# Feed forward 0 on inputs that hold the token scale, its relu on ScalarE, and a quarter of the S5 table pieces made in embedding stage 0

## Chip, cores and metric

The kernel runs on one core of one Trainium2 chip. The metric is the device time of one execution in microseconds (us): of three runs of the kernel before, the median is 2734.46 (2730.87 to 2736.14). One execution was taken with the hardware profiler; all views come from it.

Engines are called as in the profile: PE is TensorE's matmul, PEld its weight load, DVE is VectorE, ACT is ScalarE, POOL is GpSimd, and SP is SyncE, which here only issues DMAs.

## Reference

A decoder of two layers on 1024 tokens with 1024 channels. What matters here is the feed forward part of layer 0, the embedding part behind it, and the S5 mixer of layer 1, whose tables are made from parameters alone:

```python
def rms_norm(x, g):
    return x * lax.rsqrt(jnp.mean(x * x, axis=-1, keepdims=True) + RMS_EPS) * g

def sqrelu_mlp(hn, ffn_up, ffn_down):
    return jnp.square(jax.nn.relu(hn @ ffn_up)) @ ffn_down

for i in range(DEPTH):
    h = h + mix_fns[i % 2](rms_norm(h, norm_mix[i]), *mix_params[i])   # 0: RWKV and conv, 1: S5
    h = h + sqrelu_mlp(rms_norm(h, norm_ffn[i]), *ffn[i])
    gate = jax.nn.sigmoid(rms_norm(h, norm_ple[i]) @ ple[i][0])
    h = h + (p[i] @ ple[i][1]) * gate
```

In `rms_norm` the factor of a token (the token scale, `rstd` in the kernel) is one number per token; the gain `g` is one number per channel. The S5 mixer builds, per group, powers of `lam_bar` times `b_bar` and `c` (`s5_mixer` of the reference); the kernel keeps them as tables in DRAM.

## The kernel before

Channels lie on partitions and tokens along the free dimension, in two halves of 512 tokens (`hf` 0 and 1). `h[j][hf]` is a tile of 128 channels by 512 tokens. A product in float32 is made of three matmuls (`mm3`, L161): each operand is split into a high part (`prh`, `whi`, `uwh`, `hidh`) and the rest (`prl`, `wlo`, `uwl`, `hidl`), and high x high, high x rest and rest x high are added up in PSUM. ScalarE casts the high parts; DVE or POOL subtracts for the rest.

**The stages** in the trace are: mixer 0 (0 to 719 us), feed forward 0 (719 to 1500), embedding stage 0 (1500 to 1616), the S5 mixer with its gates (to 1912), feed forward 1 (to 2570) and embedding stage 1 with the output.

**Feed forward** (`ffn`, L238). In feed forward 0 and 1 the order of PE is the order in which the code issues matmuls; the order on the other engines is made by the scheduler. The work is cut into blocks of 8 steps. A block holds one group of up products (`u_run`, tile `ps_up`, 24 matmuls) and one group of down products (`d_run`, L348): seven products of Strassen's kind in the order X, Z, X, Y, X, Y, X, three matmuls each into `ps_dnx`, `ps_dny`, `ps_dnz`. Behind each product DVE adds the tile to the residual (L365; `h<-h,...` and `ha<-ha,...`, as the two halves are named in the profile). There is one tile for X, so the next X product waits until that addition has read it. There are 60 blocks with both groups, and a plain tail of four.

Beside them, at steps given by small tables of numbers, run the operations that prepare a later block:

- the up weights: `u_load` (SP, L261), the cast `u_hi` (ACT, L265) and the rest `u_lo` (POOL, L268);
- the down weights: `d_load` (SP, L276), four sums of blocks in `d_sums` (POOL, L281 to L284), the cast `d_hi` (ACT, L288) and the rest `d_lo` (DVE, L291), at the four steps of `FFN_D`;
- the operands of the down products (`operands`, L315): `relu()` reads `ps_up`, takes the maximum with 0 and multiplies with the token scale on DVE (L319); the squares are ACT's (L322, L323); four differences of squares (L333, one of them on POOL) are cast by ACT (L335), and the rests (L327) are DVE's, where one goes to POOL.

So the up products of feed forward 0 and 1 run on inputs that have the gain but not the token scale, which the relu adds. The scale of half 0 is known before feed forward 0 begins (`r0`); that of half 1 is computed in its first steps.

**The inputs of feed forward 0** are made by `done` in `prep` (L170): ACT casts h times gain (`prh`, L180), DVE makes the rest (`prl`, L181), sixteen pairs, called from `inputs` in `hook`.

**The S5 tables** are also made in feed forward 0: small operations on DVE first (`s5_tables`), then 32 pieces, a new one every `S5_EACH` = 12 steps. A piece (`s5_piece`, L1110) takes on POOL CL, tmp, their sum, sk and kt (L1126, L1127, L1133, L1158, L1160); on DVE two products and their sum (L1130, L1132, L1135); on PE two transposes into `ps_bl` (L1145) and two matmuls into `ps_k` (L1153); on ACT two copies and `brep`; and four DMAs to DRAM, three of them on SP (s5w from CL twice, L1140, and `toep` from kt, L1166). To each piece belongs a phase (`s5_phases`, L1190): four POOL operations (L1199 to L1203) on one buffer, and a DMA on SP (L1205). For every eight pieces there is one `s5_powers` on POOL, for every four one `s5_front` with its loads on SP, two transposes into `ps_c` and six small DVE operations.

**Embedding stage 0** (`ple`, L423) multiplies with the gate weights (tile `ps_g`), loads weights by SP (L148), casts them on ACT (L151) and takes their rest on DVE (L152). `side` is a list of generators, of which some are advanced behind each finished tile; before, it is empty. Here PE's order, too, is the scheduler's.

Of the kernel before, what the change touches and what calls it, by code (L numbers as in the profile page):

```python
# [5 lines left out]
F32 = mybir.dt.float32  # L6
F32R = mybir.dt.float32r
AF = mybir.ActivationFunctionType
ALU = mybir.AluOpType
# [3 lines left out]
P = 128  # L13
T = 1024
D = 1024
ND = D // P
H = 512
# [3 lines left out]
S5_START, S5_PREP, S5_AT, S5_EACH = -24, 1, 88, 12  # L21
# [7 lines left out]
FFN_D = (0, 2, 5, 7)  # L29
# [32 lines left out]
class Trunk:  # L62
# [107 lines left out]
    def prep(self, gain, split=True, eng=None, known={}, late=False):  # L170
# [4 lines left out]
        def done(j, hf):  # L175
            nc = self.nc
            s = self.hv(j, hf)
            if split:
# [10 lines left out]
        return st, done  # L189

# [19 lines left out]
    def rstd_steps(self, *accs, pool=None, tag="m"):  # L210
# [22 lines left out]
        yield out  # L233

# [3 lines left out]
    def ffn(self, l, xn, rstd, done, hook):  # L238
# [54 lines left out]
        def u_run(k):  # L293
# [8 lines left out]
            for hf in first:  # L302
# [12 lines left out]
        def operands(k, s, n, ps, hf, st, plain):  # L315
            r = st["f%d" % n] = self.np_.tile([P, H], F32, tag="sq", name="r_up", bufs=4)

            def relu():
                V.scalar_tensor_tensor(r, ps, 0.0, rstd[hf], ALU.max, ALU.mult)  # L319
# [573 lines left out]
    def s5_tables(self, pool, sp, keep_p):  # L893
# [167 lines left out]
        sq, rj = t("sq", (2, 64)), t("rj", (2, 64))  # L1061
        for k in range(9):
            o = lv[:, k - 2] if k >= 2 else (rj, ri)[k]
# [46 lines left out]
    def s5_piece(self, pc, pool):  # L1110
# [19 lines left out]
        V.tensor_mul(BL, bcc(LR[:, :, 0:8], 8), bck(Bb[0], 8))  # L1130
        yield
        V.tensor_mul(tmp3, bcc(LI[:, :, 0:8], 8), bck(Bb[1], 8))  # L1132
# [453 lines left out]
    def build(self, layers=(0, 1), stop=None):  # L1586
        tc, nc = self.tc, self.nc
        from contextlib import ExitStack
        with ExitStack() as st:
# [28 lines left out]
            for l in range(2):  # L1618
# [9 lines left out]
                with ExitStack() as s2:  # L1628
# [3 lines left out]
                    if l == 0:  # L1632
                        def tables():
                            with tc.tile_pool(name="s5tmp", bufs=1, reuse_waits="tile") as tp:
                                yield from self.s5_tables(tp, s5q, s5p)
                            t5 = s2.enter_context(tc.tile_pool(name="s5tab", bufs=1, reuse_waits="tile"))
                            self.kt = t5.tile([P, NG, 240], F32, name="kt")
                            nc.gpsimd.memset(self.kt, 0.0)
                            self.t5 = t5
                            yield  # L1640

                        def lazy(f, n):

                            yield from f(n, self.t5)

# [12 lines left out]

                        def hook(at, ffn_in=st, ffn_done=done):
                            at(-6, 2, lambda: inputs(ffn_in, ffn_done))  # L1660
                            at(-5, 6, lambda: next(ffn_in["r"]))
                            at(-4, 4, lambda: scale1(ffn_in))
                            def start(s):
# [5 lines left out]
                            for n in range(64 // NG):  # L1669
                                s0 = S5_AT + S5_EACH * n  # L1670
                                gs = [(lazy(self.s5_piece, n), S5_STEPS), (lazy(self.s5_phases, n), S5_PH)]
                                if n % 8 == 0:
                                    gs.append((lazy(self.s5_powers, n // 8), S5_POW))
                                if NG * n % 8 == 0:
                                    gs.append((lazy(self.s5_front, NG * n // 8), S5_FRONT))
# [77 lines left out]
```

## Time and profile before

| what | us |
|---|---|
| median of three runs | 2734.46 |
| the profiled execution, its own time | 2731.33 |
| the span of its records | 2729.6 |
| mean granted clock of PE | 0.978 |
| feed forward 0, first ps_up to the last block's first ps_dnz | 719.4 to 1472.4 |
| feed forward 1, the same two | 1912.7 to 2562.0 |
| embedding stage 0, ps_g | 1499.9 to 1615.9 |

The profiled execution lies inside the runs' range. A window's row gives for each engine the busy time and, in brackets, the count of instructions, then PE's granted clock as a share of full speed, the DMA engines' busy share and GB/s. A group's row gives busy time and the mean of one in ns, then the engine's idle time right before, with what ended it. A wait's row gives the sum, the number and the longest.

### The profile page before, as it was taken

What the parts mean: (1) busy time and instruction counts of PE and PEld (TensorE: products, weight loads), DVE (VectorE), ACT (ScalarE), POOL (GpSimd) and SP (SyncE); (2) the same over time, 40 slices, a digit from 0 to 9 for tenths busy, and PEclk for the clock granted to TensorE, in tenths of its full rate; (3) what the DMA queues carried; (4) which work ended last, traced back from release to release, by engine and by line L of the source; (5) the groups of instructions that cost most, each with busy time, mean ns of one, the idle gap of its engine ahead of it and who ended that gap; (6) DMA issues with size and microseconds to landing.
All of it is one profiled execution on the core that took longest, in us unless ns stands there. A gap on an engine that the chain in (4) does not pass through costs nothing.

```text
span 2729.6 us, 46656 instructions
## 1 busy us (share of the span) xinstructions
PE 2589.0 (95%) x18781; PEld 2068.6 (76%) x18781; DVE 1873.7 (69%) x2684; ACT 980.3 (36%) x1635; POOL 1172.6 (43%) x1516
## 2 busy tenths in 40 slices
PE   8998999999889989999999997999999999999998
PEld 6776777777667767777777876788788888888786
DVE  6664666663897788888888549523577787777854
ACT  4344444443422223333334336413333232233432
POOL 5444343443468895555554107311334334343400
PEclk9998999999989999999999989999999999999999
DMA  4223221321212223222222225211111111111121
GB/s 113 60 63 106 71 64 45 107 68 63 80 49 70 84 81 85 76 80 77 79 76 64 77 74 155 74 47 47 43 55 47 55 51 51 54 48 55 47 74 62
DMA packets 273428, 189.04 MB, mean 69 GB/s; under 512 B 33038, under 2 KB 256508, under 8 KB 273212
## 3 DMA queue, kind: packets, MB, share of 16 engines
q1 hardware_dynamic: 264336, 174.50, 21.8%
q10 hardware_dynamic: 7516, 7.10, 0.8%
q0 software_dynamic: 1360, 4.46, 0.5%
q8 instruction: 147, 2.41, 0.4%
q14 instruction: 69, 0.57, 0.1%
HBM read 156.92 MB, written 29.10 MB: 68 GB/s over the span
## 4 chain that ended last, share of the span: by engine, by line
PE 51%; DVE 6%; POOL 6%; issue 3%; DMA 1%; ACT 1%; POOLq 0%; SPq 0%; ACTq 0%; DVEq 0%
PE ps_dnx L362 10%; PE ps_up L163 6%; PE ps_up L165 6%; PE ps_up L164 6%; PE ps_dny L362 5%; PE ps_dnz L362 2%; PE ps_gl L163 2%; PE ps_gl L164 2%; PE ps_gl L165 2%; PE ps_g L163 2%; PE ps_g L165 2%; PE ps_g L164 2%; DVE ha L365 1%; POOL zs L1276 1%; DVE hidl L327 1%
## 5 line engine op out<-in xcount | busy, mean ns | idle before, releaser
L163 PE MATMUL ps_up<-prh,uwh 128*128 128x512 f32 x1024 | 407.4, 398 | 1.3 <-ACT prh L180 1.3
L164 PE MATMUL ps_up<-prl,uwh 128*128 128x512 f32 x1024 | 406.5, 397 | 1.7 <-DVE prl L181 1.6
L165 PE MATMUL ps_up<-prh,uwl 128*128 128x512 f32 x1024 | 406.9, 397 | 0.5 <-POOL uwl L268 0.5
L268 POOL TENSOR_TENSOR uwl<-uraw,uwh 128x512 fp32r<-128x512 f32 x136 | 184.4, 1356 | 187.9 <-ACT uwh L265 185.7
L281 POOL TENSOR_TENSOR draw<-draw 128x128 f32<-128x128 f32 x120 | 68.5, 571 | 402.0 <-DMA draw<-in_l_ffn_down_dram 354.6
L362 PE MATMUL ps_dnx<-hidh,whi 128*128 128x512 f32 x480 | 199.2, 415 | 43.9 <-DVE ha L365 30.1
L164 PEld LDWEIGHTS ps_up<-prl,uwh 128*128 128x128 f32 x1024 | 194.4, 190 | 49.5 <-DVE prl L181 4.8
L163 PEld LDWEIGHTS ps_up<-prh,uwh 128*128 128x128 f32 x1024 | 195.0, 190 | 47.1 <-ACT prh L180 1.8
L165 PEld LDWEIGHTS ps_up<-prh,uwl 128*128 128x128 f32 x1024 | 194.7, 190 | 46.0 <-POOL uwl L268 0.9
L365 DVE TENSOR_TENSOR h<-h,ps_dnx 128x512 f32<-128x512 f32 x240 | 164.3, 684 | 73.5 <-PE ps_dnx L362 72.6
L152 POOL TENSOR_TENSOR wlo<-wraw,whi 128x1024 fp32r<-128x1024 f32 x66 | 158.3, 2399 | 123.4 <-ACT whi L151 119.7
L202 POOL TENSOR_TENSOR acc<-acc,sq 128x512 f32<-128x512 f32 x70 | 105.0, 1507 | 220.8 <-ACT sq L201 217.7
L265 ACT CAST uwh<-uraw 128x512 fp32r<-128x512 f32 x136 | 84.3, 620 | 321.3 <-PE ps_up L164 307.9
L362 PE MATMUL ps_dnx<-hidl,whi 128*128 128x512 f32 x480 | 191.1, 398 | 4.6 <-DVE hidl L327 4.6
L362 PE MATMUL ps_dnx<-hidh,wlo 128*128 128x512 f32 x480 | 190.6, 397 | 0.5 <-DVE wlo L291 0.5
L163 PE MATMUL ps_z<-prh,whi 128*128 128x512 f32 x416 | 179.3, 431 | 7.4 <-ACT whi L151 6.6
L365 DVE TENSOR_TENSOR ha<-ha,ps_dnx 128x512 f32<-128x512 f32 x240 | 163.4, 681 | 24.1 <-PE ps_dnx L362 24.1
L165 PE MATMUL ps_z<-prh,wlo 128*128 128x512 f32 x416 | 166.9, 401 | 6.6 <-POOL wlo L152 6.5
L151 ACT CAST whi<-wraw 128x1024 fp32r<-128x1024 f32 x104 | 108.8, 1047 | 172.6 <-PE ps_z L164 59.4
L164 PE MATMUL ps_z<-prl,whi 128*128 128x512 f32 x416 | 165.7, 398 | 0.9 <-DVE prl L488 0.9
L322 ACT ACTIVATE hidh<-r_up 128x512 fp32r<-128x512 f32 x98 | 62.0, 632 | 278.5 <-DVE r_up L319 276.5
L327 DVE TENSOR_TENSOR hidl<-r_up,hidh 128x512 fp32r<-128x512 f32 x188 | 153.3, 828 | 12.7 <-ACT hidh L335 6.9
(441 smaller groups left out, 6340.5 us busy)
## 6 DMA issues: line engine op xcount, KB each, us to landing
uraw<-in_l_ffn_up_dram SPq DMA_DIRECT2D x128, 256.0 KB
draw<-in_l_ffn_down_dram SPq DMA_DIRECT2D x120, 256.0 KB
wraw<-in_l_w_in_dram SPq DMA_DIRECT2D x52, 512.0 KB
s5w<-s5w SPq DMA_DIRECT2D x32, 384.0 KB
wraw<-in_l_w_out_dram SPq DMA_DIRECT2D x16, 512.0 KB
wraw<-in_l_ple_gate_dram SPq DMA_DIRECT2D x16, 512.0 KB
wraw<-in_l_glu_w_dram SPq DMA_DIRECT2D x16, 512.0 KB
toep<-kt SPq DMA_DIRECT2D x32, 240.0 KB
```

Source lines behind the costliest of these rows:

```text
L151: nc.scalar.copy(hi[:, :n], raw[:, :n])
L152: self.lo_engine().tensor_sub(lo[:, :n], raw[:, :n], hi[:, :n].bitcast(F32))
L163: nc.tensor.matmul(ps, wh, xh, start=start, stop=False)
L164: nc.tensor.matmul(ps, wh, xl, start=False, stop=False)
L165: nc.tensor.matmul(ps, wl, xh, start=False, stop=stop)
L202: (eng or nc.vector).tensor_add(acc, acc, sq)
L265: A.copy(uw[m][0], raws["u"])
L268: nc.gpsimd.tensor_sub(uw[m][1], raws["u"], uw[m][0].bitcast(F32))
L281: G.tensor_add(raw[:, 4], raw[:, 0], raw[:, 2])
L327: return lambda: eng.tensor_sub(st[nm][1], t, st[nm][0].bitcast(F32))
L362: nc.tensor.matmul(ps, w[:, a], v, start=id(ps) not in begun, stop=n == 2, skip_group_check=True)
L365: V.tensor_add(hv, hv, ps)
```

## The change

**Inputs that hold the scale.** A new helper `scaled` makes an input as xs = h x gain x scale (DVE), a cast of it (ACT) and a subtraction (DVE). Half 0 gets its inputs this way from the start. Half 1 has them plain for the first four up groups; once its scale is known, `again` makes its eight input pairs a second time into the same tiles. Where the inputs hold the scale, `relu()` is one ACT operation without a scale, in feed forward 0 alone.

**S5 pieces.** A piece begins every 16 steps and not 12, 24 of them in feed forward 0. The last eight, with one set of powers and two fronts, are passed to embedding stage 0 as `side`, with tiles of their own (and a second clearing of kt). `FFN_D` becomes (0, 0, 3, 7). In `s5_piece` the two product tiles trade places, so that BL is written one step later.

```diff
-S5_START, S5_PREP, S5_AT, S5_EACH = -24, 1, 88, 12
+S5_START, S5_PREP, S5_AT, S5_EACH, S5_FFN = -24, 1, 88, 16, 24
-FFN_D = (0, 2, 5, 7)
+FFN_D = (0, 0, 3, 7)
...
-            if split:
+            if split and hf in known:
+                st["xn"][hf][j] = self.scaled(s, gain, j, known[hf])
+            elif split:
...
+    def scaled(self, s, gain, j, rstd, xn=None):
+        nc = self.nc
+        xn = xn or self.pair(self.prp, [P, H], "pr")
+        t = self.np_.tile([P, H], F32, tag="sq", name="xs", bufs=4)
+        nc.vector.scalar_tensor_tensor(t, s, self.c(gain, j), rstd, ALU.mult, ALU.mult)
+        nc.scalar.copy(xn[0], t)
+        nc.vector.tensor_sub(xn[1], t, xn[0].bitcast(F32))
+        return xn
...
-                        operands(k, FFN_RELU[hf != first[0]], 2 * q + hf, ps, hf, st, m >= NU - 4)
+                        operands(k, FFN_RELU[hf != first[0]], 2 * q + hf, ps, hf, st, m >= NU - 4, l == 0 and (hf == 0 or m >= 4))
...
             def relu():
-                V.scalar_tensor_tensor(r, ps, 0.0, rstd[hf], ALU.max, ALU.mult)
+                if scaled:
+                    A.activation(r, ps, AF.Relu)
+                else:
+                    V.scalar_tensor_tensor(r, ps, 0.0, rstd[hf], ALU.max, ALU.mult)
...
-        V.tensor_mul(BL, bcc(LR[:, :, 0:8], 8), bck(Bb[0], 8))
-        yield
-        V.tensor_mul(tmp3, bcc(LI[:, :, 0:8], 8), bck(Bb[1], 8))
+        V.tensor_mul(tmp3, bcc(LR[:, :, 0:8], 8), bck(Bb[0], 8))
+        yield
+        V.tensor_mul(BL, bcc(LI[:, :, 0:8], 8), bck(Bb[1], 8))
...
+                        def again(ffn_in, j):
+                            self.scaled(self.hv(j, 1), "l0_norm_ffn", j, ffn_in["rstd"][1], ffn_in["xn"][1][j])
...
                             at(-4, 4, lambda: scale1(ffn_in))
+                            for j in range(ND):
+                                at(-3, 2 * j + j // 4 * 5, lambda j=j: again(ffn_in, j))
...
-                            for n in range(64 // NG):
-                                s0 = S5_AT + S5_EACH * n
...
+                            for n in range(S5_FFN):
+                                for g, steps in pieces(n):
                                     for s in steps:
-                                        at(0, s0 + s, lambda g=g: next(g, 0))
+                                        at(0, S5_AT + S5_EACH * n + s, lambda g=g: next(g, 0))
...
-                        self.ple(l, st2["xn"], rstd, pt, done1, [])
+                        side = []
+                        if l == 0:
+                            clear(s2.enter_context(tc.tile_pool(name="s5tab2", bufs=1, reuse_waits="tile")))
+                            side = [(S5_EACH * n + s, g) for n in range(S5_FFN, 64 // NG) for g, steps in pieces(n) for s in steps]
+                            side = [g for _, g in sorted(side, key=lambda q: q[0])]
+                        self.ple(l, st2["xn"], rstd, pt, done1, side)
```

(`pieces` gives the generators of a piece with their steps, as the loop did before; one small computation inside `s5_tables` also no longer writes over its own input.)

Three places show what the scheduler makes of it. A row has the line, the operation and the tiles; lines of the changed kernel are some 15 higher.

DVE at the start of feed forward 0, where the last inputs are made, before:

```order
L181 SCALAR_TENSOR_TENSOR prl<-h,cv_359,prh 128x512 x4
L181 SCALAR_TENSOR_TENSOR prl<-ha_8851,cv_359,prh 128x512
L181 SCALAR_TENSOR_TENSOR prl<-ha_8852,cv_359,prh 128x512
L181 SCALAR_TENSOR_TENSOR prl<-ha_8853,cv_359,prh 128x512
L181 SCALAR_TENSOR_TENSOR prl<-ha_8854,cv_359,prh 128x512
L223 RECIPROCAL rs_9026<-sd_9024 128x4
```

and of the change:

```order
L184 SCALAR_TENSOR_TENSOR prl<-h,cv_359,prh 128x512 x4
L199 SCALAR_TENSOR_TENSOR xs<-ha_8851,cv_359,rstd 128x512
L199 SCALAR_TENSOR_TENSOR xs<-ha_8852,cv_359,rstd 128x512
L201 TENSOR_TENSOR prl<-xs,prh 128x512
L199 SCALAR_TENSOR_TENSOR xs<-ha_8853,cv_359,rstd 128x512
L201 TENSOR_TENSOR prl<-xs,prh 128x512
L199 SCALAR_TENSOR_TENSOR xs<-ha_8854,cv_359,rstd 128x512
L201 TENSOR_TENSOR prl<-xs,prh 128x512 x2
L236 RECIPROCAL rs_9042<-sd_9040 128x4
L199 SCALAR_TENSOR_TENSOR xs<-h,cv_359,rstd 128x512
L954 TENSOR_SCALAR lre<-ps_lam 128x64
L199 SCALAR_TENSOR_TENSOR xs<-h,cv_359,rstd 128x512 x2
```

Each input of half 0 (`ha`) takes two operations where it took one, and behind the reciprocal, which belongs to the scale of half 1, its eight inputs (`h`) come a second time, among the first small operations of the S5 tables.

DVE in the late blocks, around one piece (BL, tmp), before:

```order
L365 TENSOR_TENSOR h<-h,ps_dny 128x512
L319 SCALAR_TENSOR_TENSOR r_up<-ps_up,rstd 128x512
L365 TENSOR_TENSOR h<-h,ps_dnx 128x512
L327 TENSOR_TENSOR hidl<-r_up,hidh 128x512
L1130 TENSOR_TENSOR BL<-LR,Bb 128x256
L319 SCALAR_TENSOR_TENSOR r_up<-ps_up,rstd 128x512
L1135 TENSOR_TENSOR BL<-BL,tmp_13771 128x256
L365 TENSOR_TENSOR ha_8847<-ha_8847,ps_dny 128x512
L365 TENSOR_TENSOR h<-h,ps_dnx 128x512
L1132 TENSOR_TENSOR tmp_13931<-LI,Bb 128x256
```

and of the change:

```order
L383 TENSOR_TENSOR ha_8848<-ha_8848,ps_dnz 128x512
L1151 TENSOR_TENSOR BL<-LI,Bb 128x256
L383 TENSOR_TENSOR ha_8847<-ha_8847,ps_dnx 128x512
L1154 TENSOR_TENSOR BL<-BL,tmp_13573 128x256
L1122 TENSOR_TENSOR w<-bx,Fi 128x128
L383 TENSOR_TENSOR h<-h,ps_dny 128x512
L1121 TENSOR_TENSOR Bb<-bx,Fr 128x128 x2
L1123 TENSOR_TENSOR Bb<-Bb,w 128x128
L1122 TENSOR_TENSOR w<-bx,Fi 128x128
L1123 TENSOR_TENSOR Bb<-Bb,w 128x128
L383 TENSOR_TENSOR h<-h,ps_dnx 128x512
L1149 TENSOR_TENSOR tmp_13826<-LR,Bb 128x256
```

The relus (L319) no longer stand between the additions (L365, now L383); the three operations of a piece and those of a front still do.

SP in embedding stage 0 before, from the second load of the projection on:

```order
L148 DMA wraw<-in_l_ple_gate_dram 128x8x128 x4
L148 DMA wraw<-in_l_ple_proj_dram 128x2x512
L148 DMA wraw<-in_l_ple_gate_dram 128x8x128 x4
```

and of the change:

```order
L1224 DMA s5w_87<-phase 128x256
L149 DMA wraw<-in_l_ple_proj_dram 128x2x512
L1224 DMA s5w_88<-phase 128x256
L149 DMA wraw<-in_l_ple_gate_dram 128x8x128
L1102 DMA craw<-in_l_c_re_dram 128x64
L1103 DMA craw<-in_l_c_im_dram 128x64
L1102 DMA craw<-in_l_c_im_dram 128x64
L1103 DMA craw<-in_l_c_re_dram 128x64
L1224 DMA s5w_89<-phase 128x256
L149 DMA wraw<-in_l_ple_gate_dram 128x8x128
L1159 DMA s5w_85<-CL 64x2x128 x2
L1224 DMA s5w_90<-phase 128x256
```

Transfers of the tables, which wait for POOL, now stand in SP's queue between the loads of the gate weights.

More of the change, by code (lines that the diff above doesn't have):

```diff
@@ L1668, in hook @@
                             at(0, S5_START, lambda: start(S5_START))
-                            for n in range(64 // NG):
-                                s0 = S5_AT + S5_EACH * n
[L1671 to L1675, printed above, removed]
-                                for g, steps in gs:
+                            for n in range(S5_FFN):
+                                for g, steps in pieces(n):
                                     for s in steps:
-                                        at(0, s0 + s, lambda g=g: next(g, 0))
+                                        at(0, S5_AT + S5_EACH * n + s, lambda g=g: next(g, 0))
                     with tc.manual_schedule(engines={mybir.EngineType.PE}):
```

16 lines of the change are left out of this document (13 added, 3 removed).

## The prediction

> **What bounds the kernel now.** I read the page first, then busy time by windows, then the starts of one tile, then waits, groups and the timeline inside feed forward 0.
>
> ```profile
> span 2729.6 us, 46656 instructions
> ## 1 busy us (share of the span) xinstructions
> PE 2589.0 (95%) x18781; PEld 2068.6 (76%) x18781; DVE 1873.7 (69%) x2684; ACT 980.3 (36%) x1635; POOL 1172.6 (43%) x1516
> ```
>
> PE is busy for 95% of the span, so the change can only win where PE is not at its pace. The next view compares three windows of feed forward 0 (its start, its early blocks, its late blocks) with a steady window of feed forward 1 and one of embedding stage 0.
>
> ```profile
> core 0: us, PE busy (x) PEld busy (x) DVE busy (x) ACT busy (x) POOL busy (x), PEclk, DMA share, GB/s
> 719.00:816.00 97.00, 83.76 (x328) 63.00 (x329) 89.96 (x208) 35.23 (x58) 58.37 (x85) 0.89 0.18 48
> 816.00:1018.00 202.00, 182.14 (x759) 144.07 (x758) 153.13 (x203) 57.17 (x94) 181.09 (x332) 0.95 0.27 77
> 1018.00:1473.00 455.00, 434.90 (x1928) 348.93 (x1927) 377.41 (x547) 150.81 (x270) 234.96 (x343) 0.99 0.29 78
> 2000.00:2520.00 520.00, 520.00 (x2252) 422.40 (x2250) 397.70 (x562) 159.68 (x237) 200.33 (x274) 1.00 0.17 51
> 1530.00:1613.00 83.00, 83.00 (x363) 67.45 (x362) 46.06 (x64) 26.22 (x39) 0.00 (x0) 1.00 0.17 50
> ```
>
> In feed forward 1 PE never rests: 520.00 / 2252 = 0.231 us per matmul. A block has 45 matmuls, so its floor is 10.39 us. Feed forward 0 issues the same blocks; their first product into ps_dnz, and the first ps_up of each stage, give its real pace.
>
> ```profile
> L163 PE MATMUL ps_up<-prh,uwh x41: 388/388/632, 719.4 to 757.8; 128*128 128x512 f32 x41
> ```
> ```profile
> L163 PE MATMUL ps_up<-prh,uwh x50: 388/393/477, 1912.7 to 1959.0; 128*128 128x512 f32 x50
> ```
> ```profile
> L362 PE MATMUL ps_dnz<-hidh,whi x5: 394/397/397, 758.4 to 815.5; 128*128 128x512 f32 x5
> ```
> ```profile
> L362 PE MATMUL ps_dnz<-hidh,whi x5: 390/392/393, 1944.9 to 1990.1; 128*128 128x512 f32 x5
> ```
> ```profile
> L362 PE MATMUL ps_dnz<-hidh,whi x40: 388/397/632, 1018.1 to 1472.4; 128*128 128x512 f32 x40
> ```
>
> Three losses follow. **Start**: 815.5 - 719.4 = 96.1 us, against 1990.1 - 1912.7 = 77.4 in feed forward 1: 18.7 over. **Early**, 16 intervals: 1018.1 - 815.5 = 202.6 against 166.2: 36.4 over. **Late**, 39 intervals: 454.3 against 405.2: 49.1 over. Embedding stage 0 has no loss at all: PE is busy 83.00 of 83.00, and POOL does nothing there.
>
> **Late blocks.** What PE waits for, and the DVE groups of that window:
>
> ```profile
> PE ps_dnx L362 <- DVE ha L365: 13.6, 16, 1.9
> PE ps_dnx L362 <- DVE h L365: 6.4, 3, 2.8
> ```
> ```profile
> L319 DVE SCALAR_TENSOR_TENSOR r_up<-ps_up,rstd 128x512 f32<-128x512 f32 x40 | 27.6, 690 | 7.4 <-PE ps_up L165 7.3
> ...
> L1135 DVE TENSOR_TENSOR BL<-BL,tmp 128x256 f32<-128x256 f32 x25 | 20.9, 835 | 0.2
> ...
> L1132 DVE TENSOR_TENSOR tmp<-LI,Bb 128x256 f32<-128x256 f32 x24 | 12.8, 534 | 0.5
> L1130 DVE TENSOR_TENSOR BL<-LR,Bb 128x256 f32<-128x256 f32 x25 | 12.3, 493 | 7.6 <-DMA s5w<-BL 7.6
> ```
> ```profile
> 1155.88 0.61 PE L1153 MATMUL ps_k<-CL,brep 128*128 128x128 f32 x4
> 1156.25 0.48 PE L362 MATMUL ps_dnx<-hidh,whi 128*128 128x512 f32 x1
> 1156.56 0.40 PE L362 MATMUL ps_dnx<-hidl,whi 128*128 128x512 f32 x1
> ```
>
> PE waits only for DVE's additions: the next X product needs the tile back. The table pieces also cost PE itself: from 1155.88 to 1156.56 are 0.68 us where 0.231 are due, so ps_k costs 0.45; ps_bl has half as many matmuls, so about 0.22, together 0.67 a piece. For 25 pieces that is 16.8 us, which leaves 49.1 - 16.8 = 32.3 us of stall. DVE is loaded with 377.41 / 39 = 9.68 us per block, against PE's 10.39 + 0.43 = 10.82, or 89%. In feed forward 1 it is 397.70 / 520.00 = 76.5%, without a stall.
>
> The change takes the 40 relus away (27.6 us) and, with a piece every 16 steps and not every 12, a quarter of the pieces' three operations (12.3 + 12.8 + 20.9 = 46.0, so 11.5). DVE is left with (377.41 - 27.6 - 11.5) / 39 = 8.67 us, and PE's floor becomes 10.39 + 0.50 x 0.67 = 10.73: 81%. On a straight line between 76.5% (no stall) and 89% (32.3), 81% gives 11 us. After: 39 x 0.335 + 11 = 24 over, so **-25**. Bounds: all stall goes (-36); or stall falls only with the pieces, to three quarters (-12).
>
> The relu on ScalarE is not in this trace. Its nearest rows are ScalarE's reading of PSUM and its function pass at the same size, both in embedding stage 0:
>
> ```profile
> L450 ACT ACTIVATE g_ple<-g_ple 128x512 f32<-128x512 f32 x15 | 9.2, 627 | 17.7 <-DVE g_ple L449 17.7
> ...
> L231 ACT COPY rstd<-ps_rs 128x512 f32<-128x512 f32 x2 | 1.2, 586 | 0.6 <-PE ps_rs L229 0.6
> ```
>
> So 0.59 to 0.63 us, I take 0.63: 25 us for 40 in the late window, on an engine busy 150.81 of 455. It rises to 39%, and I cost it at nothing; PE's next block covers it. If the relu sat behind a waiting whi on ScalarE, that cover would be gone; the early window is where it could.
>
> **Early blocks.** Here POOL is busy 181.09 of 202.00, mostly with phases, made for all 32 pieces in this stretch.
>
> ```profile
> ACT whi L288 <- POOL draw L284: 30.1, 12, 4.1
> ```
> ```profile
> 816.00:1018.00 202.00, 50.62 (x88) 0.95 0.27 77
> ```
> ```profile
> L1200 POOL TENSOR_TENSOR pt<-E,E 128x256 f32<-128x256 f32 x29 | 21.8, 751 | 0.9
> ```
> ```profile
> 856.10 1.30 POOL L333 TENSOR_TENSOR r_up<-r_up 128x512 f32<-128x512 f32 x1
> ...
> 857.43 1.14 ACT L335 CAST hidh<-r_up 128x512 fp32r<-128x512 f32 x2 [4.85 <-POOL r_up L333]
> ...
> 858.60 2.03 DVE L327 TENSOR_TENSOR hidl<-r_up,hidh 128x512 fp32r<-128x512 f32 x2 [3.62 <-ACT hidh L335]
> ...
> 861.28 0.80 PE L362 MATMUL ps_dnx<-hidh,whi 128*128 128x512 f32 x1 [3.67 <-DVE h L365]
> ```
>
> The second fence is POOL's work on the tile phase alone; with pt it is 72 us for 29 phases, 2.5 each. The last fence is how it reaches PE: a late POOL difference holds ScalarE, ScalarE holds DVE's hidl, and the addition queued behind that holds PE for 3.67. I put nearly the whole 36.4 - 4 (six pieces on PE) = 32 on this. By the order of the change, phases come just as densely beside the up weights' casts, but 24 of them end at cast 23, not 27: 4 of 16 blocks are freed, **-9** (8, and 1 for fewer pieces). Bounds: 0, and -25 if DVE's load matters here as in the late blocks.
>
> FFN_D moves the whi cast two steps up, from 5 to 3 (2.6 us), and the sums of the weights are still POOL's; whi will wait longer on ScalarE, with relus and squares behind it. The wait is 2.5 us on average now. I take 0 and bound it by half of those waits reaching PE, +15.
>
> **Start.** DVE is busy 89.96 of 97.00 here. The change adds 16 multiplications and 16 subtractions for 8 operations that go: 24 more, less four relus. The nearest rows are the operation that makes prl, early and later in this stretch:
>
> ```profile
> L181 DVE SCALAR_TENSOR_TENSOR prl<-h,cv,prh 128x512 fp32r<-128x512 f32 x5 | 6.6, 1361 | 0.3 <-ACT prh L180 0.3
> ```
> ```profile
> L181 DVE SCALAR_TENSOR_TENSOR prl<-ha,cv,prh 128x512 fp32r<-128x512 f32 x4 | 2.7, 740 | 0.0
> ```
>
> All 24 at these prices are 18 to 33 us, less 4 x 0.69 = 2.8, so 15 to 30 net. Not all is paid: the window has 7 us of DVE idle, and in the order the small table operations have gone behind the inputs. Between the lower net less that idle, 8, and a third of the upper, 10, I take **+9**. Bounds: +3 (half of the lower net, less some idle) and +18.
>
> The added operations read two tiles of SBUF, the relus that go read PSUM. [...]
>
> **Embedding stage 0.** Eight pieces come here: 8 x 0.67 + 0.5 for two front transposes = **+6** on PE, which had no gap. In front of ps_k PE now stands in order behind POOL's CL.
>
> ```profile
> 944.66 2.67 DMA s5w<-phase
> ```
> ```profile
> L1133 POOL TENSOR_TENSOR CL<-CL,tmp 128x288 f32<-128x288 f32 x26 | 21.2, 816 | 0.2
> ...
> L1160 POOL TENSOR_TENSOR kt<-kt,sk 128x32 f32<-128x32 f32 x27 | 10.7, 398 | 0.6 <-POOL uwl L268 0.6
> ```
>
> A piece is three operations like the first and two like the second on POOL, 3.2 us, and a phase of 2.5, whose single buffer is free again 2.67 us after its transfer starts. Eight of both are 46 us in a stage of 116 that gave POOL nothing. By the order, PE reaches the first ps_k some 150 matmuls (35 us) behind the stage's first ps_g, and then one per 32 matmuls, 7.4 us. POOL needs 3.2 + 2.5 = 5.7 us a piece where nothing holds it, so it keeps up: I take **+4** for one or two single waits, bounds 0 and +37 (the slower rival below).
>
> **Sum** against the profiled execution (2731.33): -25 - 9 + 9 + 6 + 4 = -15, so **2716**. That execution is 3.1 below the median of the runs, 2734.46, within their spread (2730.87 to 2736.14); I add nothing for it.
>
> **Rivals.** *More gain (DVE decides everywhere).* Relief in the early blocks as in the late: -34 and -20, start +9, rest +10: **2696**. For it: hidl and the additions are DVE's. Against: POOL at 90%.
> *Nothing in all.* Late only the lower bound (-12), early 0 because phases lie as densely as before, start +9, embedding +6: +3, **2734**. For it: POOL stays dense, and the additions are held by single long operations ahead of them (hidl took 2.03 us for two), not by DVE's mean load.
> *Slower: embedding stage 0 is paced by POOL.* If phase, landing and piece follow one another, a piece is 2.5 + 2.67 + 0.4 (issue, an estimate) + 3.2 = 8.8 us, and a third longer where weight loads share SP, 12. Against PE's 7.4 that is 8 x 4.6 = +37 in place of +4. It ends at 2716 + 33 = **2749**. It decides from 28 us of such waits up (2716 - 4 + 28 = 2740), that is from 10.9 us a piece. For it: one buffer for the phases, and SP issues their transfers in order with weight loads. Against it: POOL has those 35 us of lead.
> *The change doesn't do what it says* is ruled out by its order: 62 relus stand on ScalarE, 24 pieces in feed forward 0, 8 after it; feed forward 1 keeps its order.
>
> **How the numbers follow.** Forecast 0.52 (2704 to 2727), more gain 0.18, nothing 0.16 (2723 to 2742), slower 0.14 (2740 to 2755). A measurement of this kernel tells about 0.2%, 5.5 us, from no change, so "same" is 2729 to 2740. Faster: 0.50 + 0.18 + 0.04 = 0.72; slower: 0.13; same: 0.15. The range 2688 to 2740 leaves out the slower case and the far end of the gain.
>
> **What would show it.** After: late blocks at 11.0 us, not 11.65, and DVE near 81% of them; early blocks still 12 us or more up to about the twelfth; start near 105 us; in embedding stage 0 at most 10 us of PE waiting, at ps_k, released by POOL's CL. Wrong if PE still waits for DVE's additions in the late blocks as before, if the whi cast holds ScalarE in front of a relu, or if ps_g loses its unbroken row.

## The result, and the profile after

The changed kernel takes 2712.43 us (median of four runs, 2711.90 to 2715.64), the kernel before 2735.3 beside it: a ratio of 0.9926, with a 95% interval of 0.9914 to 0.9938. The forecast was 2716. The profiled execution took 2712.81 with a span of 2711.0, 18.6 less than before. The windows view of the changed kernel shows the same four stretches as before, in the same columns (length, busy time of PE, PEld, DVE, ACT, POOL with the count, PE's granted clock, DMA share, GB/s):

```profile
719.00:831.00 112.00, 84.52 (x329) 64.60 (x328) 100.01 (x223) 46.53 (x76) 50.88 (x76) 0.88 0.15 39
831.00:1024.00 193.00, 177.00 (x753) 140.23 (x752) 136.77 (x188) 65.36 (x107) 161.84 (x278) 0.97 0.25 74
1024.00:1443.00 419.00, 419.00 (x1881) 342.26 (x1880) 316.64 (x477) 165.91 (x285) 208.35 (x304) 1.00 0.27 75
1470.00:1600.00 130.00, 124.41 (x579) 101.04 (x578) 82.37 (x119) 46.71 (x83) 67.40 (x115) 0.99 0.36 97
```

The late blocks (third row) now have PE busy for all 419.00 us; the view of waits is empty for PE there. The start (first row) is longer, and embedding stage 0 (last row) has PE idle for 5.6 us. Cut at the starts of the fifth, twenty-first and sixtieth block's first ps_dnz and of the first ps_g and ps_gl, as in the prediction:

| stretch, us | before | predicted change | after | change |
|---|---|---|---|---|
| start, first ps_up to the fifth block | 96.1 | +9 | 109.9 | +13.8 |
| early, 16 intervals | 202.6 | -9 | 192.8 | -9.8 |
| late, 39 intervals | 454.3 | -25 | 419.5 | -34.8 |
| first ps_g to first ps_gl (embedding stage 0 and the S5 mixer) | 228.4 | +10 | 242.9 | +14.5 |

The rest of the 18.6 is in stretches that the change leaves alone, 1 to 3 us each. So every stretch moved the way that was forecast. Whether it did so for the reasons given is what the experiments ask.

### The profile page after: what moved, and what is told of

Same layout as the page of the kernel before. It is cut to its first block, busy times and chain, and to the rows that moved or that the text cites. A ratio compares the mean times of both kernels' runs of the same rounds, so it can differ in the third digit from the quotient of the medians.

```text
span 2711.0 us, 46747 instructions
## 1 busy us (share of the span) xinstructions
PE 2579.0 (95%) x18781; PEld 2069.7 (76%) x18781; DVE 1822.1 (67%) x2646; ACT 1022.0 (38%) x1705; POOL 1175.4 (43%) x1517
## 4 chain that ended last, share of the span: by engine, by line
PE 57%; POOL 7%; DVE 4%; issue 2%; DMA 2%; ACT 1%; POOLq 0%; ACTq 0%; SPq 0%; DVEq 0%
PE ps_dnx L380 11%; PE ps_up L164 7%; PE ps_up L166 7%; PE ps_up L165 7%; PE ps_dny L380 5%; PE ps_dnz L380 3%; PE ps_gl L164 2%; PE ps_gl L166 2%; PE ps_gl L165 2%; PE ps_g L164 2%; PE ps_g L165 2%; PE ps_g L166 2%; DMA draw<-in_l_ffn_down_dram 1%; DVE prl L184 1%; POOL zs L1295 1%
## 5 line engine op out<-in xcount | busy, mean ns | idle before, releaser
L166 PEld LDWEIGHTS ps_up<-prh,uwl 128*128 128x128 f32 x1024 | 194.2, 190 | 45.2
L383 DVE TENSOR_TENSOR h<-h,ps_dnx 128x512 f32<-128x512 f32 x240 | 164.6, 686 | 85.0 <-PE ps_dnx L380 84.3
L380 PE MATMUL ps_dnx<-hidh,whi 128*128 128x512 f32 x480 | 193.0, 402 | 23.8 <-DVE ha L383 20.7
L383 DVE TENSOR_TENSOR ha<-ha,ps_dnx 128x512 f32<-128x512 f32 x240 | 163.7, 682 | 15.3 <-PE ps_dnx L380 15.3
L383 DVE TENSOR_TENSOR ha<-ha,ps_dny 128x512 f32<-128x512 f32 x120 | 82.5, 687 | 108.8 <-PE ps_dny L380 108.7
```

The costliest lines, as they stand in the source:

```text
L166: nc.tensor.matmul(ps, wl, xh, start=False, stop=stop)
L380: nc.tensor.matmul(ps, w[:, a], v, start=id(ps) not in begun, stop=n == 2, skip_group_check=True)
L383: V.tensor_add(hv, hv, ps)
```

## The experiments

Twelve kernels ran, e9_less_pool and e10_less_dve with two runs each, the others with four or more. The table gives for each the median, its ratio to the runs of before beside it with the interval, and the four stretches of the profiled execution, cut as above.

| kernel | median | ratio (95%) | start | early | late | ps_g to ps_gl |
|---|---|---|---|---|---|---|
| before | 2734.46 | | 96.1 | 202.6 | 454.3 | 228.4 |
| the change | 2712.43 | 0.9926 (0.9914, 0.9938) | 109.9 | 192.8 | 419.5 | 242.9 |
| e1_all32 | 2748.02 | 1.0057 (1.0040, 1.0074) | 109.2 | 199.9 | 455.9 | 230.7 |
| e2_split_only | 2699.43 | 0.9883 (0.9868, 0.9898) | 96.5 | 189.6 | 419.1 | 243.7 |
| e3_old_d | 2714.51 | 0.9942 (0.9926, 0.9959) | 109.3 | 192.8 | 419.2 | 241.8 |
| e4_no_swap | 2711.45 | 0.9926 (0.9912, 0.9941) | 109.3 | 192.7 | 419.4 | 242.0 |
| e5_aligned12 | 2727.05 | 0.9975 (0.9966, 0.9984) | 96.9 | 196.6 | 451.9 | 229.9 |
| e6_offset4 | 2723.16 | 0.9961 (0.9947, 0.9975) | 109.2 | 191.7 | 426.1 | 241.7 |
| e7_later | 2712.19 | 0.9920 (0.9905, 0.9935) | 106.5 | 192.0 | 419.3 | 241.3 |
| e8_split_ph | 2699.21 | 0.9873 (0.9858, 0.9888) | 96.3 | 175.5 | 438.1 | 241.6 |
| e9_less_pool | 2717.30 | 0.9934 (0.9911, 0.9956) | 97.4 | 196.3 | 446.1 | 230.2 |
| e10_less_dve | 2711.97 | 0.9914 (0.9892, 0.9936) | 96.1 | 197.1 | 438.2 | 228.9 |
| e11_ph_cl | 2720.38 | 0.9949 (0.9931, 0.9966) | 96.1 | 175.9 | 456.5 | 240.1 |
| e12_24at12 | 2721.79 | 0.9955 (0.9938, 0.9971) | 96.7 | 194.2 | 442.3 | 239.6 |

### Which part of the change took the late stall away

**e1_all32** keeps scaled inputs and the relu on ScalarE, with all pieces where they were:

```diff
-S5_START, S5_PREP, S5_AT, S5_EACH, S5_FFN = -24, 1, 88, 16, 24
+S5_START, S5_PREP, S5_AT, S5_EACH, S5_FFN = -24, 1, 88, 12, 32
```

> The change with all 32 pieces in feed forward 0, one every 12 steps, none in embedding stage 0; scaled inputs and the relu on ScalarE stay. Theory A (the late stall follows DVE's mean load): DVE loses only the 27.6 us of relus in the late window, 8.97 of 10.82 us per block or 83%, so half the stall stays: late blocks 11.2 us (10.76 in the change, 11.65 before). Theory B (the relus between the additions were the stall): late blocks 10.8 us, PE's own work alone. Theory C (the pieces' spacing or BL's wait for its own transfer was the stall): at least the spacing's part comes back, 11.3 us or more. All: embedding stage 0 returns from 128.7 to 116 us; early blocks lose 4 to 9 us to the eight phases. Total: A about 2726, B about 2711.

**e2_split_only** is the other half: pieces split, inputs and relu as before.

```diff
-            if split and hf in known:
+            if False:
...
-operands(k, FFN_RELU[hf != first[0]], 2 * q + hf, ps, hf, st, m >= NU - 4, l == 0 and (hf == 0 or m >= 4))
+operands(k, FFN_RELU[hf != first[0]], 2 * q + hf, ps, hf, st, m >= NU - 4, False)
...
-                            for j in range(ND):
-                                at(-3, 2 * j + j // 4 * 5, lambda j=j: again(ffn_in, j))
```

> The change without the scaled inputs and with the relu on DVE as before: 24 pieces every 16 steps, eight in embedding stage 0, new FFN_D, BL and tmp3 swapped. Theory A: DVE at 9.38 of 10.73 us per late block, 87%, so stall 28 of 32 us, late blocks 11.45 us. Theory B: 11.55 us. Theory C: late blocks near 10.8 us. All: the start is back at 96 us (111 in the change), embedding stage 0 stays at 128 us. Total: A about 2725, B about 2729, C about 2700.

The late windows of e1_all32 and, behind it, of e2_split_only:

```profile
1030.00:1486.00 456.00, 435.16 (x1925) 349.79 (x1924) 348.36 (x509) 172.84 (x310) 246.22 (x356) 0.99 0.29 79
```
```profile
1007.00:1426.00 419.00, 419.00 (x1882) 342.45 (x1882) 340.92 (x517) 143.87 (x246) 207.61 (x304) 1.00 0.27 75
```

With the relu on ScalarE but a piece every 12 steps, a late block takes 11.69 us, as before (11.65). With the relu on DVE and a piece every 16 steps it takes 10.75, and PE never waits. So the relu's place did nothing for the late blocks, and the pieces did it all. Theories A and B fall; C holds in its part on the pieces, but none of the totals forecast for e1_all32 (2726 and 2711) came near 2748.02. The two rows also refute the prediction's measure: per block DVE is busy 348.36 / 39 = 8.93 us in the one and 340.92 / 39 = 8.74 in the other, 83% and 81% of PE's floor, and the stall beyond PE's own work is 34 us in the one and 1 in the other. (DVE's busy time holds the time by which its operations are lengthened, of which more below.)

**e4_no_swap** and **e3_old_d** undo the two small parts:

```diff
-        V.tensor_mul(tmp3, bcc(LR[:, :, 0:8], 8), bck(Bb[0], 8))
+        V.tensor_mul(BL, bcc(LR[:, :, 0:8], 8), bck(Bb[0], 8))
...
-        V.tensor_mul(BL, bcc(LI[:, :, 0:8], 8), bck(Bb[1], 8))
+        V.tensor_mul(tmp3, bcc(LI[:, :, 0:8], 8), bck(Bb[1], 8))
```

> The change with BL and its helper tile in their old places, so that BL is written first and waits for its own transfer to DRAM on DVE (7.6 us of waiting in the late window before). Theory C: late blocks get slower, 11.0 us or more instead of 10.76, and PE waits for DVE's additions again. Theories A and B: no change, 10.76 us, total 2712 to 2714.

```diff
-FFN_D = (0, 0, 3, 7)
+FFN_D = (0, 2, 5, 7)
```

> The change with the old steps of the down weights, FFN_D = (0, 2, 5, 7). If the new steps matter, early blocks or the start get slower by 3 us or more (12.05 us per early block in the change); if they are covered, as the prediction has it, everything is within 2 us and the total at 2712.

Both leave every stretch within 1.2 us of the change's. So BL's wait for its transfer and the steps of the down weights are not what moved the time.

### Spacing, count or place

Every second piece of the kernel before began in the middle of a block. Two kernels test that place. **e5_aligned12** (on e2_split_only) begins each piece at a block's first step, 12 steps apart on average:

```diff
-S5_START, S5_PREP, S5_AT, S5_EACH, S5_FFN = -24, 1, 88, 16, 24
+S5_START, S5_PREP, S5_AT, S5_EACH, S5_FFN = -24, 1, 88, 12, 32
-S5_STEPS = (0, 2, 4, 6, 7, 10, 12)
+S5_STEPS = (0, 2, 4, 6, 7, 8, 8)
...
-                                        at(0, S5_AT + S5_EACH * n + s, lambda g=g: next(g, 0))
+                                        at(0, S5_AT + 8 * (n + n // 2) + s, lambda g=g: next(g, 0))
```

> Built on e2_split_only (plain inputs, relu on DVE), with all 32 pieces in feed forward 0 again at 12 steps apart on average, but alternately 8 and 16, so that each begins on a block's first step; a piece's last two parts come 2 and 4 steps earlier so that it is done before the next. Theory P (position: before, every second piece began in the middle of a block, and there its DVE operations stand in front of the addition that the next X product waits for): late blocks 10.8 to 10.9 us, PE's own work; embedding stage 0 116 us; total about 2690. Theory L (the load or the mean spacing decides): DVE is as loaded as before, late blocks 11.65 us as before; total about 2725.

**e6_offset4** begins all of them in the middle, 16 apart (88 becomes 92 in the change):

> The change with its pieces still 16 steps apart but each begun four steps later, in the middle of a block. Theory P: every piece meets the place that every second one met before; 32 us of stall for some 13 such pieces are 2.5 us each, 19 pieces in the late blocks give 48 us, late blocks about 12.0 us, total about 2760. Theory L: 10.76 us, total 2712.

Theory P falls as the main cause: aligned pieces at 12 steps stall nearly as before (11.59 us a block), and pieces in the middle at 16 steps take only 10.93. In e5_aligned12 the pieces are 8 and 16 steps apart by turns, so that kernel alone doesn't separate place from nearness; e6_offset4 does. Its waits of PE in the late window:

```profile
PE ps_dnx L380 <- DVE ha L383: 2.3, 5, 0.5
PE ps_dnx L380 <- DVE h L383: 0.9, 3, 0.3
```

Eight waits are left, 3.2 us together. The place is not free, though: the profiled execution of e6_offset4, 2713.64, is the fastest of five with a median of 2723.16, so its stretches show too little, and by the medians it is some 10 us slower than the change (the two intervals do not meet). Theory P's forecast of 2760 was 37 us off, theory L's 2712 was 11 off.

**e12_24at12** is e2_split_only with one number changed (16 becomes 12 in S5_EACH): as many pieces in the stage, closer together.

> As e2_split_only (24 pieces in feed forward 0, eight in embedding stage 0, plain inputs, relu on DVE), but with the 24 pieces 12 steps apart as before, so that they end some twelve blocks before the stage's end. The count of pieces is that of e2_split_only; only their spacing differs. If spacing decides: blocks with pieces run at 11.6 us as before, the last twelve at 10.4, 39 late blocks take about 438 us (419 in e2_split_only), total about 2718. If the smaller count decides: late blocks take 419 to 424 us, total near 2700.

Two windows of its late part, with pieces and behind the last piece:

```profile
1020.00:1370.00 350.00, 335.88 (x1482) 270.39 (x1481) 286.51 (x414) 114.67 (x201) 171.00 (x250) 0.99 0.27 74
1380.00:1450.00 70.00, 70.00 (x305) 56.91 (x304) 51.69 (x73) 19.59 (x30) 23.68 (x34) 1.00 0.17 53
```

While there are pieces, PE is idle for 14 of 350 us; as soon as they have ended it is idle for none, with the relu on DVE all along. The late blocks take 442.3 us, not 419.1; the forecast for spacing was 438 and a total of 2718 (2721.79 measured), for the count 419 to 424 and 2700. So blocks with pieces at 12 steps stall as before, and a smaller count only shortens the stretch in which they do. **Of the 35.2 us that the pieces are worth in the late blocks (454.3 to 419.1), 12.0 come with fewer pieces at the old spacing and 23.2 with the wider spacing.** The split is not a clean one: the late stretch holds 25 pieces before, 17 in e12_24at12 and 19 in e2_split_only, and 12.0 includes PE's own work for eight pieces. Eight pieces had to leave the stage to make room for the wider spacing. A closer spacing also puts more table work into each block; that DVE's mean load is not what decides is shown by e1_all32, not by this pair.

### What a piece does at 12 steps

The longest late block of the kernel before, from the timeline of DVE, of POOL and of PE (start, duration, engine and line, tiles; in brackets the idle time before, and what ended it). The first row is the same DVE operation at a place where POOL does nothing:

```profile
768.12 1.28 DVE L327 TENSOR_TENSOR hidl<-r_up,hidh 128x512 fp32r<-128x512 f32 x2
1245.81 3.45 DVE L327 TENSOR_TENSOR hidl<-r_up,hidh 128x512 fp32r<-128x512 f32 x2
1249.18 0.28 DVE L1103 TENSOR_TENSOR w<-bx,Fi 128x128 f32<-128x128 f32 x1
1249.38 0.67 DVE L365 TENSOR_TENSOR h<-h,ps_dnx 128x512 f32<-128x512 f32 x1
```
```profile
1245.70 1.34 POOL L327 TENSOR_TENSOR hidl<-r_up,hidh 128x512 fp32r<-128x512 f32 x1
1247.14 1.57 POOL L268 TENSOR_TENSOR uwl<-uraw,uwh 128x512 fp32r<-128x512 f32 x1
```
```profile
1250.11 0.80 PE L362 MATMUL ps_dnx<-hidh,whi 128*128 128x512 f32 x1 [2.78 <-DVE h L365]
1250.70 0.63 PE L362 MATMUL ps_dnx<-hidl,whi 128*128 128x512 f32 x1
1251.12 0.63 PE L362 MATMUL ps_dnx<-hidh,wlo 128*128 128x512 f32 x1
```

Two hidl operations on DVE take 3.45 us beside POOL's hidl and uwl, and end 0.55 us behind the latter; without POOL two take 1.28. The addition stands behind them (and behind w, an operation of a front), PE waits 2.78 us, and then its matmuls are 0.63 us instead of 0.39 at a granted clock of 0.50, as the windows of 2 us there show:

```profile
1248.00:1250.00 2.00, 0.00 (x0) 0.00 (x0) 2.00 (x4) 0.00 (x0) 0.70 (x1) 0.86 0.05 13
1250.00:1252.00 2.00, 1.89 (x5) 1.52 (x6) 1.55 (x6) 0.59 (x1) 0.00 (x0) 0.50 0.33 32
1252.00:1254.00 2.00, 2.00 (x6) 1.63 (x5) 1.74 (x4) 0.35 (x1) 0.00 (x0) 0.50 0.48 69
1254.00:1256.00 2.00, 2.00 (x6) 1.54 (x6) 1.13 (x2) 0.00 (x0) 0.00 (x0) 0.50 0.34 102
```

The block from 1237.5 takes 16.6 us. Of the nineteen waits in the late blocks two were followed by a granted clock of 0.50, this one (up to 1256) and one of 1.81 us (from 1109.5 to 1112.5); behind five others of 1.7 to 1.9 us it stayed at 1.00. So the length of a wait alone does not explain it, and what does is not shown by these runs.

This block is no exception. In the late blocks of the kernel before, 75 DVE operations take over 200 ns longer than the same operation at its shortest, and every one of them runs beside a POOL operation; the 314 that read PSUM (L365, L319) all take 0.67 to 0.69 us. In 18 of the 19 waits of PE, the DVE operations that follow one another without a pause up to the addition have together lost at least as much as PE waits (to 0.01 us). In e2_split_only 47 operations are still lengthened (the mean of hidl is 855 ns, its shortest in the kernel before 0.68 us), and PE never waits, so it is not their number alone that counts, but where they stand in the queue.

Two kernels take work out of the piece at 12 steps. **e9_less_pool** drops four of its five POOL operations, **e10_less_dve** two of its three on DVE (both on the kernel before):

```diff
-        G.tensor_mul(tmp, bcc(LI, 9), bck(X[1], 9))
...
-        G.tensor_add(CL, CL, tmp)
...
-        G.tensor_mul(sk, self.dT[:, gs].rearrange("p (g o) -> p g o", o=1).broadcast_to([P, NG, 16]),
-                     self.eye16.rearrange("p (o c) -> p o c", o=1).broadcast_to([P, NG, 16]))
-        G.tensor_add(kt[:, :, 112:128], kt[:, :, 112:128], sk)
```

> The kernel before (a piece every 12 steps, all 32 in feed forward 0) without four of the five POOL operations of a piece: CL is only its first product, and the diagonal is not added to kt, so the tables are incomplete. POOL loses 2.45 of 3.2 us a piece, DVE, PE and the DMAs keep all they had. Theory S (DVE operations that read two tiles are stretched beside POOL's, and the addition behind them comes late): BL's addition falls from 835 to near 420 ns, the differences on DVE from 1016 to about 860, late blocks from 11.65 to 11.0 us or less. Theory Q (DVE's queue itself is too full at 12 steps): late blocks stay at 11.5 us or more.

```diff
-        V.tensor_mul(tmp3, bcc(LI[:, :, 0:8], 8), bck(Bb[1], 8))
...
-        V.tensor_add(BL, BL, tmp3)
```

> The kernel before without two of the three DVE operations of a piece (BL is only its first product, so the tables are incomplete); POOL keeps all. Theory S: hidl, wlo and the differences still collide with POOL, so only a part of the stall goes: late blocks 11.2 to 11.4 us. Theory Q: DVE has 33.7 us less in the late window, 76% of a block's time, late blocks 10.8 to 10.9 us.

BL's addition in e9_less_pool and in e2_split_only, from the groups of DVE in the late window:

```profile
L1133 DVE TENSOR_TENSOR BL<-BL,tmp 128x256 f32<-128x256 f32 x26 | 22.4, 861 | 0.2
```
```profile
L1154 DVE TENSOR_TENSOR BL<-BL,tmp 128x256 f32<-128x256 f32 x19 | 7.9, 418 | 0.0
```

Less POOL work takes 8.2 us from the late blocks (446.1), and the mean of the addition stays at 861 ns. The timeline of e9_less_pool shows beside what it runs; one addition in the middle of a block, and the wait of PE behind it:

```profile
1150.48 1.33 POOL L268 TENSOR_TENSOR uwl<-uraw,uwh 128x512 fp32r<-128x512 f32 x1
1150.69 1.40 DVE L1133 TENSOR_TENSOR BL<-BL,tmp 128x256 f32<-128x256 f32 x1
1155.85 0.47 PE L362 MATMUL ps_dnx<-hidh,whi 128*128 128x512 f32 x1 [1.28 <-DVE ha L365]
```

In this kernel the additions of about 1.4 us all stand beside uwl, POOL's work for the up weights, and end 0.28 us behind it. Most of those of 0.5 to 0.9 us, at a block's start, stand beside CL's first product, the one POOL operation of a piece that this kernel keeps. With nothing on POOL at their start they take 0.42. So the longest are not made by the piece's own POOL work. In the kernel before, nine additions of BL stand beside uwl, and each is followed within 6 us by a wait of PE, with DVE at work all the time between (9.4 us of waits out of 20.0); the three in the middle of a block that do not meet uwl are followed by none.

Less DVE work takes 16.1 us (438.2), half of the stall. The waits of PE left in e10_less_dve:

```profile
PE ps_dnx L362 <- DVE ha L365: 4.4, 5, 3.1
PE ps_dnx L362 <- DVE h L365: 3.3, 3, 2.4
```

These are eight, where there were nineteen. Neither theory has both numbers: e9_less_pool, at 11.44 us a block, lies near Q's 11.5 and not at S's 11.0, and e10_less_dve, at 11.24, lies in S's range (11.2 to 11.4) and not in Q's (10.8 to 10.9). POOL's mean load decides as little as DVE's: e9_less_pool has 171.39 us of POOL work in the late window and stalls, e2_split_only has 207.61 and doesn't.

At 16 steps the same addition takes 418 ns in e2_split_only and 425 in e6_offset4, where uwl begins only 0.33 to 0.42 us after it. The stall is thus made where DVE operations, a piece's and a front's among them, meet POOL's in front of an addition that PE needs. That is read from the traces of these kernels; the meetings differ from kernel to kernel (in e5_aligned12 no addition of BL meets uwl, and hidl and the fronts meet POOL instead). Why 16 steps avoid nearly all meetings that matter is not settled. Second buffers for the piece's tiles would test whether pieces block one another; no run has them.

### The early blocks

**e8_split_ph** (on e2_split_only) lets POOL make a phase only behind a piece:

```diff
-        E = pool.tile([P, 2, 16, 8], F32, tag="s5p", name="phase", bufs=1)
+        E = pool.tile([P, 2, 16, 8], F32, tag="tmp", name="phase", bufs=1)
-S5_PH = (1, 2, 4)
+S5_PH = (3, 4, 6)
```

> Built on e2_split_only; the phase takes the buffer of tmp, so that POOL can make one phase only behind each piece (one in 16 steps) and no longer all in a row. If the row of phases on POOL is what the early blocks wait for, they fall from 189.6 us for 16 to about 176 (PE's own work and clock), total about 2686. If it is DVE or the table operations, they stay within 4 us of 189.6, and late blocks may lose a little to the phases: total 2697 to 2705.

**e11_ph_cl** does the same with CL's buffer (tag "CL", S5_PH = (11, 12, 13), S5_POW = (0, 1, 2, 3, 4, 5, 6)):

> As e8_split_ph, but the phase takes CL's buffer and not tmp's, so that it is made only behind PE's ps_k, in the block without DVE work for a piece; the powers move to where they still precede it. The early blocks should again gain some 14 us over e2_split_only (175 for 16). If the 19 us that the phases cost in the late blocks of e8_split_ph came from where they stood beside DVE's work, late blocks come back from 11.23 towards 10.75 us, total about 2686; if any POOL work there costs it, they stay near 11.2 and the total near 2699.

Early blocks of e2_split_only and of e8_split_ph:

```profile
817.00:1007.00 190.00, 175.94 (x753) 139.96 (x752) 147.49 (x199) 57.21 (x92) 151.93 (x264) 0.98 0.25 74
```
```profile
815.00:990.00 175.00, 171.23 (x749) 137.22 (x749) 141.76 (x199) 56.40 (x91) 92.76 (x132) 1.00 0.24 67
```

POOL falls from 151.93 to 92.76 us, PE's idle time from 14 to 3.8, and the mean granted clock rises from 0.98 to 1.00. So the row of phases on POOL is what the early blocks wait for, as the prediction had it. But the phases have to go somewhere: spread over the late blocks they cost 19 us there in e8_split_ph, and 37 in e11_ph_cl, which moves the powers too. The totals forecast missed: 2686 for e8_split_ph by 13 us, and for e11_ph_cl both 2686 and 2699, by 34 and 21.

### The start

**e7_later** moves the matmuls of half 1's scale six steps later and remakes half 1's inputs from up group 10 on. (By then h has been added to, so these inputs hold a part of the feed forward's own result.)

```diff
-                            at(-5, 6, lambda: next(ffn_in["r"]))
-                            at(-4, 4, lambda: scale1(ffn_in))
+                            at(-4, 4, lambda: next(ffn_in["r"]))
+                            at(-3, 2, lambda: scale1(ffn_in))
...
-                                at(-3, 2 * j + j // 4 * 5, lambda j=j: again(ffn_in, j))
+                                at(10-6 + j // 4, 1 + 2 * (j % 4), lambda j=j: again(ffn_in, j))
...
-l == 0 and (hf == 0 or m >= 4)
+l == 0 and (hf == 0 or m >= 10)
```

> The change with the matmuls of half 1's token scale six steps later, and half 1's inputs remade from up group 10 on, not 4 (three more relus on DVE). If the start is lost to PE standing behind POOL's sum of squares (8.3 us at ps_ms) and to DVE behind the remade inputs, the stretch from the first ps_up to the fifth ps_dnz falls from 111 us to 102 or less, total about 2704. If it is lost to the sixteen operations more before the first products, it stays at 109 to 112.

The waits of PE in the change's start, and DVE behind the reciprocal:

```profile
PE ps_ms L232 <- POOL acc L215: 8.3, 1, 8.3
PE ps_dnx L380 <- DVE ha L383: 7.0, 5, 2.5
PE ps_dnx L380 <- DVE hidl L345: 5.1, 1, 5.1
```
```profile
744.12 0.17 DVE L236 RECIPROCAL rs<-sd 128x4 f32<-128x4 f32 x1
752.47 0.82 DVE L199 SCALAR_TENSOR_TENSOR xs<-h,cv,rstd 128x512 f32<-128x512 f32 x1 [8.18 <-ACT rstd L244]
```

In the change PE stands 8.3 us at ps_ms, in front of the up products behind it, until POOL has the sum of squares; then DVE stands 8.18 us at the first remade input until PE and ACT have made the scale from it. With both moved, the start takes 106.5 us instead of 109.9, between the two forecasts, and the median does not change. The 3.4 us are won behind the first ps_dnz. Up to it, from the first ps_up, e7_later takes 49.5 us and the change 49.4, where e2_split_only, with plain inputs, takes 39.7. So some 10 us belong to the scaled inputs ahead of the first ps_dnz, and moving half 1's does not cure that. PE still waits there in e7_later (2.8 us at ps_ms, 2.8 for prl, 2.4 for wlo); how much each of the added operations costs was not separated.

## Why the prediction was right, and where it was not

- **The total** (2716 against 2712.43) and the sign were right, and all four stretches moved the way that was forecast. That the sum came so near is in part luck: the late blocks gained 9.8 us more than forecast, and the start and embedding stage 0 lost 9.3 us more.
- **Late blocks** (forecast -25, bounds -12 and -36; measured -34.8): the step that failed is the straight line from DVE's mean load to the stall. It gave the relus 27.6 of the 39.1 us of relief and so most of the gain. The relus are worth nothing here (e1_all32: 455.9 against 454.3), and the pieces are worth the whole. The lower bound of the prediction (-12), a stall that falls with the pieces' count, is near what fewer pieces at the old spacing give (12.0 in e12_24at12, though with 17 pieces in the late stretch and not 19); the other 23.2 come with the spacing, which no term of the sum had. What the line should have asked is which lengthened DVE operation stands in front of an addition that PE waits for. Also, the line knew no clock: behind two of the waits PE ran at a granted clock of 0.50.
- **Relu on ScalarE** (taken at 0.63 us and at no cost): 40 of them in the late window took 23.8 us, 0.595 each, on an engine 40% busy (165.91 of 419), and the waits view has no engine waiting for them. Right, but they bought nothing.
- **Early blocks** (forecast -9, measured -9.8): size and cause held. The prediction freed the last four of the sixteen intervals, for 8 us: between the starts of ps_dnz they fell from 53.3 to 45.2. e8_split_ph shows the cause; e2_split_only gains 13.0, so the scaled inputs give 3.2 of it back.
- **FFN_D at nothing**: held (e3_old_d).
- **Start** (forecast +9, bounds +3 and +18; measured +13.8): right sign, mis-sized. The working counted DVE's operations, which fits the 10 us ahead of the first ps_dnz; it left out that the remade inputs wait for a scale, in DVE's queue and in PE's, and what stands behind them there (3.4 us come back in e7_later). The 32 added operations, in the start window of the change:

```profile
L201 DVE TENSOR_TENSOR prl<-xs,prh 128x512 fp32r<-128x512 f32 x16 | 11.9, 764 | 0.1
L199 DVE SCALAR_TENSOR_TENSOR xs<-ha,cv,rstd 128x512 f32<-128x512 f32 x8 | 8.8, 1117 | 1.2 <-POOL acc L215 1.2
L199 DVE SCALAR_TENSOR_TENSOR xs<-h,cv,rstd 128x512 f32<-128x512 f32 x8 | 6.1, 778 | 8.2 <-ACT rstd L244 8.2
```

  They took 26.8 us, 0.84 each. The upper of the prediction's two prices, 1361 ns, was paid by four (1632 to 1853 ns, beside POOL's uwl or acc).
- **Embedding stage 0** (forecast +10; measured +12.7 from the first ps_g to the last, and +14.5 to the first ps_gl, behind the S5 mixer): both terms held in size. PE's busy time in the stage rises by 7.9 us, of which 1.7 are a stretch of 3.4 us at a granted clock of 0.50 (around 1487), so 6.2 are work (forecast 6). Its waits in the change:

```profile
PE ps_ms L232 <- POOL acc L215: 2.3, 1, 2.3
PE ps_g L166 <- DVE wlo L153: 1.6, 1, 1.6
PE ps_pp L164 <- DVE g_ple L467: 0.9, 1, 0.9
PE ps_bl L1164 <- ACT rstd L244: 0.6, 1, 0.6
```

  They sum to 5.4 us, where the stage had 1.7 before, so the +4 is about there, but not where it was put: none is at ps_k. The prediction's sign of being wrong, a ps_g row that is no longer unbroken, did come. The half clock was in no term. The rival that POOL paces the stage did not happen; POOL is busy 67.40 of 130 us. No run shows its third more for weight loads on SP; its 0.4 us for an issue was an estimate, and the 29 issues of phases in the early blocks of before have a median of 0.34 us. Phase, landing and piece did not follow one another: the eight phases begin 4.7 us apart on average (1490.8 to 1523.7), the eight ps_k 8.2 us (1515.7 to 1572.8).

So the forecast came near although it credited a good part of the gain to the wrong half: the pieces bring about -35 in the late blocks and cost about 15 in embedding stage 0, and the scaled inputs with the relu on ScalarE cost 12 to 13 in all (a median of 2712.43 against 2699.43, each beside its own runs of before). **The version without it, e2_split_only, beats both kernels: 0.9883 (0.9868 to 0.9898) of before, where the change has 0.9926 (0.9914 to 0.9938).** e8_split_ph, at 0.9873 (0.9858 to 0.9888), can't be told from it.

## What to carry to other kernels

An engine's mean load did not tell here whether another waits for it: DVE at 81% of PE's floor for a block went with 1 us of stall (e2_split_only), at 83% with 34 us (e1_all32). Look at what stands in the queue in front of the operation that is waited for, and test the spacing of periodic side work with one number before moving main work to another engine. When a change has two parts, run each alone: here one paid for the other.

## What the runs showed of the hardware

The same DVE addition of two SBUF tiles (BL) took 418 ns on average in e2_split_only and 835 in the kernel before, 1.10 to 1.41 us in the nine cases where POOL's uwl was running, and two hidl operations took 3.45 us beside POOL instead of 1.28, while the additions and relus that read PSUM kept means of 0.68 to 0.69 us. And a wait of 2.78 us was followed by some 6 us at a granted clock of 0.50, which costs some 3 us (an estimate from the rows of 2 us), about as much again as the wait itself; one of 1.81 us was followed by 3 us of it, and the other seventeen waits of that window, 0.30 to 1.87 us, by none.
